# A modulation loaded by column halves, first products opened over them, and two operator groups moved to a later stage

## The chip, the cores and the metric

The kernel runs on one NeuronCore of a Trainium2 chip. The metric is device time in microseconds (us) of one execution. Engines are named as in the profile: PE multiplies matrices (PEld loads its weights), DVE, ACT and POOL work on tiles, SP only issues DMAs. ACT and POOL can issue DMAs too.

## The reference

Two transformer blocks run one after the other in fp32, on 256 tokens of width 1024. Only the first block's opening and the parameters of the second block's first mixer matter here.

```python
def first_block(x, c, ctx, c_ctx, ada_w, ada_b, g_mix, ...):
    ...
    for i in range(DEPTH):
        mod_lat = (silu_c @ ada_w[i] + ada_b[i])[:, None, :]
        mod_ctx = (silu_cc @ ada_w[i] + ada_b[i])[None, None, :]
        sh1, sc1, ga1, sh2, sc2, ga2 = jnp.split(mod_lat, 6, axis=-1)
        ...
        u_lat = modulate(rms_norm(h_lat, g_mix[i]), sh1, sc1)   # norm * (1 + sc1) + sh1
        u_ctx = modulate(rms_norm(h_ctx, g_mix[i]), csh1, csc1)
        if i % N_MIXERS == 0:
            ql, kl, vl = jnp.split((u_lat @ w).reshape(B, L, 3, H, dh), 3, axis=2)
            ql, qc = rms_norm(ql, na_q_gain[j]), rms_norm(qc, na_q_gain[j])
            ...
def s5_mixer(xn, w_in, lam_re, lam_im, b_re, b_im, c_re, c_im, d_skip, log_dt, w_glu):
    u = (xn @ w_in)
    a_bar = jnp.exp(lam * dt)
    b_bar = ((a_bar - 1.0) / lam)[..., None] * b_mat
    # scan: s = a_bar * s + b_bar u ;  y = Re(c_mat s) + d_skip * u ; then a gated product
```

## The kernel before

Activations lie transposed: feature tile k (128 of the 1024 features) has the latent tokens in `h[k]` and the context tokens in `hc[k]`, 256 columns each. Every fp32 operand is split in a high and a low part. For weights that is `whi` (ACT) and `wlo` (DVE), for activations `xh` (ACT) and `xl` (DVE). A product is three matmuls, `mm_x` or `mm_w`: high by high and the two mixed ones.

**The start stage** comes first. It works out the parameters of the second block's S5 mixer (class `S5`), loads and transposes the inputs, computes the shift and the scale of the first norm, norms, and splits the first weights. All of the S5 work needs only parameters, so the kernel does it where PE has little else.

- `S5.__init__` and `tables` are a serial chain of small DVE operations, with transposes on PE. `c` transposes the C matrices and copies them (`ct`, `pf`). It also builds the skip diagonal `dd`. There are four operator groups r = 0 to 3. `e(r)` builds group r's table on DVE from `pz` and `bb` through `tm`. `operators(r)` runs `k1` (`cbk` copies, products into `kp`, copied to `kt`), `et` (16 transposes, four copies, four DMAs into `edr`) and `k2` (transposes into `kst`). `save`, `k_out` and later `spread` write tables to DRAM (`cdr`, `kdr`, `tdr`). They are read again when the second block begins.
- `ada_steps(l, n)` computes modulation n (0 is shift, 1 is scale) of layer l. It has eight steps of one 512 KB row block each, and `ada(m)` runs the next m of the queue `ada_q`. The last step copies to `adacc`, transposes, and adds the bias into `mods`. For the scale it also makes `scg`.
- `rstd` sums squares on PE, takes a square root on ACT and a reciprocal on DVE, and spreads the result over the partitions. `normed` makes for each feature tile and each stream `t` (DVE), `xh` (ACT) and `xl` (DVE).

**Order.** Most of the start is inside `tc.manual_schedule`, in which each engine runs what is written, in the written order. From `w_first.append` on, a scheduler orders the instructions by its own estimate.

**After the start** comes the neighbourhood attention, stage attn0. Its first pair of heads (`lead`) makes query and key products in the PSUM buffers `g`, and the value products go to `sc`. These are 96 matmuls each. `norm(b)` then norms the heads on DVE (`ss`, `rq`, `ri`, `rt`, `qn`, `sp`), and `turn(b)` transposes them on PE into `pt`. The pool `at0`, in which these tiles lie, takes the memory of `pp`, the pool of the S5 tables, which is closed at the end of the start. **mlp0** is the first block's feed-forward. It runs one `ada_q` step between its tiles.

## Time and profile before

| what | value |
|---|---|
| runs | 1773.23 us median of 3 (1770.42 to 1775.66) |
| profiled execution | 1774.26 us, of which the span is 1772.5 us, mean granted PE clock 0.982 |
| PE | 1684.8 us busy, 95% of the span |
| DVE, ACT, POOL | 1177.6, 797.4 and 445.7 us |
| DMA | 286.57 MB, mean 162 GB/s |

PE is the busiest engine, and it is near full after the first slice of the span. The stage of the change is the first 105 us. There all engines wait for each other, so shares over the whole span say little about it. How to read the rows further down: a timeline row has the start, the length, the engine, the line, the tiles written and read, and in brackets the idle time just before with what ended it. "x16" is a run of 16 instructions in one row. A windows row lists busy times of PE, PEld, DVE, ACT and POOL in one stretch, with the granted PE clock (1.00 is 2.4 GHz), the DMA share, and GB/s.

### The profile page before, as it was taken

The numbers are of one execution on the slowest core, as the hardware profiler recorded it, in microseconds if no ns is written. First come the engines' busy times: TensorE is split into PE (matmuls) and PEld (weight loads), VectorE is DVE, ScalarE is ACT, GpSimd is POOL, SyncE is SP. The second block draws the span as 40 slices with busy tenths as digits, with TensorE's granted clock in tenths as the row PEclk, the third lists the DMA queues.
The fourth block names the chain that finished last, engine by engine and source line by source line (L and its number), as shares of the span: only waits on it lengthen the run. The fifth ranks groups of instructions, "written<-read, shape, count | busy, mean of one in ns | idle before, by whom it ended". The sixth has DMA issues, their size and how long they took to land. (4 is left out here: it accounts for less than half of the span.)

```text
span 1772.5 us, 33896 instructions
## 1 busy us (share of the span) xinstructions
PE 1684.8 (95%) x13257; PEld 1485.2 (84%) x13257; DVE 1177.6 (66%) x2412; ACT 797.4 (45%) x1463; POOL 445.7 (25%) x619
## 2 busy tenths in 40 slices
PE   6899999999999999998998999989899999999999
PEld 5687888876677777888878999979899999789998
DVE  6877777855545333447985756768577788957674
ACT  5544444434323131324674635536444465544453
POOL 4022112146897000040002000221431322424130
PEclk9899999999999999999999999999999999999999
DMA  9566455333766555332206666698459574335952
GB/s 283 180 161 193 123 153 169 91 112 130 238 197 214 160 173 151 87 95 72 84 25 167 189 187 186 209 310 228 129 149 247 146 224 143 108 103 166 233 160 90
DMA packets 428288, 286.57 MB, mean 162 GB/s; under 512 B 37513, under 2 KB 405336, under 8 KB 428128
## 3 DMA queue, kind: packets, MB, share of 16 engines
q1 hardware_dynamic: 422064, 271.53, 52.8%
q0 software_dynamic: 2800, 7.29, 1.3%
q10 hardware_dynamic: 3264, 5.59, 0.9%
q8 instruction: 104, 1.70, 0.4%
q14 instruction: 56, 0.46, 0.1%
HBM read 271.41 MB, written 17.15 MB: 163 GB/s over the span
## 5 line engine op out<-in xcount | busy, mean ns | idle before, releaser
L109 ACT ACTIVATE whi<-raw 128x1024 fp32r<-128x1024 f32 (+2 forms) x388 | 390.1, 1013 | 470.4 <-PE g L295 361.5
L112 DVE TENSOR_TENSOR wlo<-raw,whi 128x1024 fp32r<-128x1024 f32 (+2 forms) x388 | 466.1, 1207 | 186.3 <-ACT whi L109 182.7
L296 PE MATMUL g<-xh,wlo 128*128 128x256 f32 (+1 forms) x1216 | 372.8, 307 | 8.0 <-DVE wlo L112 8.0
L294 PE MATMUL g<-xh,whi 128*128 128x256 f32 (+1 forms) x1216 | 371.9, 307 | 1.6 <-ACT xh L109 1.2
L295 PE MATMUL g<-xl,whi 128*128 128x256 f32 (+1 forms) x1216 | 371.5, 305 | 0.0
L294 PE MATMUL g<-oh,whi 128*128 128x256 f32 (+1 forms) x1056 | 333.2, 316 | 3.5 <-ACT oh L109 1.4
L296 PE MATMUL g<-oh,wlo 128*128 128x256 f32 (+1 forms) x1056 | 333.0, 315 | 0.0
L295 PE MATMUL g<-ol,whi 128*128 128x256 f32 (+1 forms) x1056 | 332.6, 315 | 0.4 <-DVE ol L112 0.4
L296 PEld LDWEIGHTS g<-xh,wlo 128*128 128x128 f32 x1216 | 232.2, 191 | 21.5 <-DVE wlo L112 10.2
L294 PEld LDWEIGHTS g<-xh,whi 128*128 128x128 f32 x1216 | 231.6, 191 | 17.6 <-ACT whi L109 3.9
L295 PEld LDWEIGHTS g<-xl,whi 128*128 128x128 f32 x1216 | 231.8, 191 | 10.9
L294 PEld LDWEIGHTS g<-oh,whi 128*128 128x128 f32 x1056 | 198.2, 188 | 24.2 <-issue 3.7
L295 PEld LDWEIGHTS g<-ol,whi 128*128 128x128 f32 x1056 | 198.3, 188 | 15.8 <-DVE ol L112 1.2
L296 PEld LDWEIGHTS g<-oh,wlo 128*128 128x128 f32 x1056 | 199.4, 189 | 14.3 <-issue 0.2
L302 PE MATMUL g<-whi,xh 128*128 128x256 f32 x560 | 163.1, 292 | 3.9 <-ACT whi L109 1.6
L303 PE MATMUL g<-wlo,xh 128*128 128x256 f32 x560 | 157.9, 282 | 0.1
L304 PE MATMUL g<-whi,xl 128*128 128x256 f32 x560 | 156.9, 283 | 0.2 <-DVE xl L115 0.2
L115 DVE SCALAR_TENSOR_TENSOR h<-g,mods,h 128x256 f32<-128x256 f32 x64 | 30.9, 483 | 142.2 <-PE g L296 142.2
L302 PEld LDWEIGHTS g<-whi,xh 128*128 128x128 f32 x560 | 105.9, 189 | 12.8 <-issue 8.7
L109 ACT ACTIVATE oh<-t 128x256 fp32r<-128x256 f32 (+1 forms) x108 | 51.3, 482 | 124.4 <-DVE t L112 124.4
L303 PEld LDWEIGHTS g<-wlo,xh 128*128 128x128 f32 x560 | 105.9, 189 | 0.8 <-issue 0.3
L304 PEld LDWEIGHTS g<-whi,xl 128*128 128x128 f32 x560 | 105.4, 189 | 1.3 <-issue 0.8
(329 smaller groups left out, 2823.4 us busy)
## 6 DMA issues: line engine op xcount, KB each, us to landing
raw<-mlp_w SPq DMA_DIRECT2D x128, 512.0 KB, 4.3
ada<-ada_w SPq DMA_DIRECT2D x88, 512.0 KB, 5.0
raw<-ffn_w_up SPq DMA_DIRECT2D x88, 512.0 KB, 5.2
raw<-ffn_w_down SPq DMA_DIRECT2D x32, 384.0 KB, 3.8
raw<-ffn_w_down SPq DMA_DIRECT2D x32, 320.0 KB, 3.4
raw<-na_wqkv SPq DMA_DIRECT2D x32, 256.0 KB, 5.0
raw<-a_w_glu SPq DMA_DIRECT2D x16, 512.0 KB, 7.2
raw<-w_kv SPq DMA_DIRECT2D x16, 512.0 KB, 3.7
```

Of the source, the lines that this page charges most:

```text
L109: last[0] = A.activation(out=o, in_=i, func=f, **kw)
L112: (e or V).tensor_tensor(out=o, in0=a, in1=b, op=op)
L115: V.scalar_tensor_tensor(out=o, in0=a, scalar=s, in1=b, op0=op0, op1=op1)
L294: T.matmul(ps, lhsT=a, rhs=xh[k][:, s0:s1], start=first, stop=False)
L295: T.matmul(ps, lhsT=a, rhs=xl[k][:, s0:s1], start=False, stop=False)
L296: T.matmul(ps, lhsT=b, rhs=xh[k][:, s0:s1], start=False, stop=last_)
L302: T.matmul(ps, lhsT=xh[k][:, t0:t0 + 128], rhs=a, start=first, stop=False)
L303: T.matmul(ps, lhsT=xh[k][:, t0:t0 + 128], rhs=b, start=False, stop=False)
L304: T.matmul(ps, lhsT=xl[k][:, t0:t0 + 128], rhs=a, start=False, stop=last_)
```

## The change

- The first shift and scale come as halves of their columns (`ada_half`, 256 KB per step). The first halves of both serve feature tiles 0 to 3, the second halves tiles 4 to 7.
- The norm of tiles 0 to 3 and the query and key products over them are written ahead of the second halves. The value products over them are interleaved with the second scale half. Then follow tiles 4 to 7 and the rest of both products. `operators(0)` stands between the two. All this is now inside the manual schedule. PSUM buffers `g` and `sc` stay open from the start into attn0.
- `e(0)` stands ahead of the squares' sums, `c` and the skip diagonal (`skip`) behind them. `e(1)` and `operators(1)` stand behind the last lead product.
- Groups 2 and 3 go to mlp0, between steps of `ada_q`, with `k_out` and `spread` behind them. What they need (`bb`, `pz`, `kst`) is written to `cdr` in `save` and read again by `reload` before mlp0. `save`, `et`, `k_out` and `spread` issue their DMAs on POOL now, not on ACT and SP.
- The B matrices come in one DMA each and are transposed by 32 transposes, where before there were 32 transposes and 32 products.

```diff
--- before.py
+++ after.py
+    def ada_half(l, n, j, tiles):
+
+        acc = [None]
+
+        def step(k):
+            t = tiles(k)
+            c0 = n * 1024 + j * 512
+            dma(out=t, in_=I["ada_w"][l, k * 128:(k + 1) * 128, c0:c0 + 512])
+            if k == 0:
+                acc[0] = bank("x")
+            ps = acc[0]
+            for q in range(4):
+                T.matmul(ps[32 * q:32 * q + 32, 0:128], lhsT=sl[:, k, :], rhs=t[:, 128 * q:128 * q + 128],
+                         start=k == 0, stop=k == KT - 1)
+            if k < KT - 1:
+                return
+            cp(adacc[:, 0:128], ps[:, 0:128])
+            pt = bank("x")
+            T.transpose(pt[:, 0:128], adacc[:, 0:128], ident)
+            c = n * 8 + 4 * j
+            m = mods[l][:, c:c + 4, :]
+            tt(m, pt[:, 0:128].rearrange("p (q x) -> p q x", q=4)[:, :, 0:2],
+               adab[l][:, c:c + 4].unsqueeze(2).to_broadcast([128, 4, 2]), ADD)
+            if n == 1:
+                stt(scg[l][:, 0, 4 * j:4 * j + 4, :], m, 1.0,
+                    gmix[l][:, 4 * j:4 * j + 4].unsqueeze(2).to_broadcast([128, 4, 2]), ADD, MUL)
+
+        return [lambda k=k: step(k) for k in range(KT)]
...
+            if between:
+                between()
...
-                for j in range(2):
-                    b_ = bt[r][j].rearrange("g (p h) -> g h p", h=16)
-                    for h_ in range(16):
-                        o_ = pb[r][64 * j:64 * j + 64, 32 * h_:32 * h_ + 32]
-                        if j:
-                            T.matmul(o_, lhsT=b_[:, h_, :], rhs=ident[0:32, 0:32])
-                        else:
-                            T.transpose(o_, b_[:, h_, :], ident[0:32, 0:32])
+                b_ = bt[r].rearrange("g (n h) -> g h n", h=16)
+                for h_ in range(16):
+                    T.transpose(pb[r][:, 32 * h_:32 * h_ + 32], b_[:, h_, :], ident[0:32, 0:32])
...
         def save(self):
             for i in range(2):
-                dma_a(out=cdr[:, 512 * i:512 * i + 512], in_=self.ct[i].rearrange("p g h -> p (g h)"))
-            dma_a(out=cdr[:, 1024:1536], in_=self.pf_.rearrange("p r t g -> p (r t g)"))
-            dma_a(out=cdr[:, 1536:1632], in_=self.ph_.rearrange("p i g -> p (i g)"))
+                G.dma_start(out=cdr[:, 512 * i:512 * i + 512], in_=self.ct[i].rearrange("p g h -> p (g h)"))
+            G.dma_start(out=cdr[:, 1024:1536], in_=self.pf_.rearrange("p r t g -> p (r t g)"))
+            G.dma_start(out=cdr[:, 1536:1632], in_=self.ph_.rearrange("p i g -> p (i g)"))
+            for i in range(2):
+                c = cdr[:, 1632:3168].rearrange("p (r x) -> p r x", r=4)
+                G.dma_start(out=c[:, :, 128 * i:128 * i + 128], in_=self.bb[i].rearrange("p (r g) h -> p r (g h)", r=4))
+                G.dma_start(out=c[:, :, 256 + 64 * i:320 + 64 * i],
+                            in_=self.pw2[i].rearrange("p (r g) t -> p r (g t)", r=4))
+                G.dma_start(out=cdr[:, 3168 + 256 * i:3424 + 256 * i],
+                            in_=self.kst[i][:, 0:2].rearrange("p r q j x -> p (r q j x)"))
 
         def e(self, r):
+            t = self.fp.tile([128, 2048], F32, tag=("e1", "e2", "em", "em")[r], name="em").rearrange(
+                "p (i q j t h) -> p i q j t h", i=2, q=4, j=2, t=8)
+            self.em[r] = [t[:, i] for i in range(2)]
+            if r < 2:
+                bb, pw2 = [x_[:, 8 * r:8 * r + 8, :] for x_ in self.bb], [x_[:, 8 * r:8 * r + 8, :] for x_ in self.pw2]
...
-                dma_a(out=edr[:, 16 * q + 4 * r:16 * q + 4 * r + 4, :], in_=et)
+                G.dma_start(out=edr[:, 16 * q + 4 * r:16 * q + 4 * r + 4, :], in_=et)
...
         def k_out(self):
             for qh in range(2):
                 for s in range(8):
-                    dma(out=kdr[:, 32 * qh:32 * qh + 32, 7 + s, :],
+                    G.dma_start(out=kdr[:, 32 * qh:32 * qh + 32, 7 + s, :],
...
+    lead = ExitStack()
+    psum_pools(lead, g=2, sc=2)
...
-            psum_pools(s0, x=5, s=3)
-            ada_pool(s0)
+            psum_more(s0, x=3, s=1)
+            adh = s0.enter_context(tc.tile_pool(name="adh", bufs=12))
...
-            halves = lambda k: [stage("l", 2 * (k // 2) + j) for j in range(2)] if k % 2 else None
-            ada_q = ada_steps(0, 0, halves) + ada_steps(0, 1, halves)
+            half = lambda k: adh.tile([128, 512], F32, tag="ada", name="ada")
+            for n in range(2):
+                ada_q.extend(ada_half(0, n, 0, lambda k, n=n: stage("l", 4 * n + k // 2) if k % 2 else half(k)))
+            for n in range(2):
+                ada_q.extend(ada_half(0, n, 1, half))
...
-                for f in sloads[7:]:
+                for f in sloads[5:]:
+                    f()
+                for f in small_loads[15:-1]:
                     f()
                 s5.tables()
-                for f in small_loads[15:-1]:
-                    f()
+                s5.tiles(pp, spare)
+                s5.e(0)
+                act(small, h[KT - 2][:, 0:1], AF.Sqrt, bias=eps, scale=0.0)
                 ada(4)
+                between = [lambda: None] * 2 + [lambda: ada(1)] * 6
+                between[3] = lambda: (prep_vectors(va), ada(1))
+                r_ = rstd(512, 0, None, "s", lambda: between.pop(0)())
                 s5.c()
-                s5.e(0)
-                ada(2)
-                act(small, h[KT - 2][:, 0:1], AF.Sqrt, bias=eps, scale=0.0)
-                r_ = rstd(512, 0, None, "s")
-                prep_vectors(va)
-                ada(3)
+                s5.skip()
+                ada(6)
+                x = new_x(xa, "x", 512, 16, 16)
+
+                def norm_k(*ks):
+                    normed(x, r_, 512, lambda k, v: scg[0][:, 0, k, v:v + 1], lambda k, v: modcol(0, 0, k, v), ks)
+
+                def lead_mm(i, k):
+                    for b in range(2):
+                        for t in range(2):
+                            mm_x(lead_ps[i][b][:, t * 256:(t + 1) * 256], w_first[i], 0, 256, x, k, (2 * b + t) * 128,
+                                 k == 0 and t == 0, k == KT - 1 and t == 1)
+
+                norm_k(0)
+                w_first = [Weights(wpairs(w, D, 0), by_k=True)]
+                norm_k(1, 2, 3)
+                lead_ps = [[bank("g"), bank("g")], [bank("sc"), bank("sc")]]
+                for k in range(4):
+                    lead_mm(0, k)
+                    ada(2)
+                w_first.append(Weights(wcols(w, 2 * D, 256), by_k=True))
+                operators(0)
+                for k in range(4):
+                    ada(2)
+                    lead_mm(1, k)
+                norm_k(4, 5, 6, 7)
+                for i in range(2):
+                    for k in range(4, 8):
+                        lead_mm(i, k)
                 s5.e(1)
-                operators(0)
-                ada(2)
-                w_first = [Weights(wpairs(w, D, 0), by_k=True)]
-                ada(2)
-                s5.e(2)
+                operators(1)
                 small_loads[-1]()
                 stt(gna, gna, 0.125, swg[:, 208:272], MUL, MUL)
                 ts(gsw[0], gsw[0], 0.125, MUL)
-                operators(1)
-                ada(3)
-            w_first.append(Weights(wcols(w, 2 * D, 256), by_k=True))
-            x = new_x(xa, "x", 512, 16, 16)
-            normed(x, r_, 512, lambda k, v: scg[0][:, 0, k, v:v + 1], lambda k, v: modcol(0, 0, k, v))
-            operators(2)
-            s5.e(3)
-            operators(3)
-            s5.zero()
-            s5.save()
-            s5.k_out()
+                s5.zero()
+                s5.save()
...
-            psum_pools(s0, g=2, sc=2, pt=2, po=1, x=1)
+            psum_more(s0, pt=2, po=1, x=1)
...
-                    return [load, mm_all, lambda: norm(0), lambda: norm(1), lambda: turn(0), lambda: turn(1)]
+                    return [load, lambda: norm(0), lambda: norm(1), lambda: turn(0), lambda: turn(1)]
...
-            ada_q[2::5] = [lambda f=f, s=s: (s5.spread(s), f()) for s, f in enumerate(ada_q[2:42:5])] + ada_q[42::5]
+            at_ = {20: s5.skip, 26: lambda: s5.e(2), 38: lambda: s5.e(3), 47: s5.k_out}
+            for n, r in ((30, 2), (42, 3)):
+                for i, f in enumerate((s5.k1, s5.et, s5.k2)):
+                    at_[n + i] = lambda f=f, r=r: f(r)
+            for n, g_ in at_.items():
+                ada_q[n] = lambda f=ada_q[n], g_=g_: (f(), g_())
+            ada_q += [lambda s=s: s5.spread(s) for s in range(8)]```

The first place is DVE where the norm begins, before. `t` is the scaled tile, `xl` its low part; `h` and `hc` are the two streams.

```order
L115 SCALAR_TENSOR_TENSOR scg_74<-mods_72,vt 128x16
L112 TENSOR_TENSOR e_506<-tm_432,tm_433 128x512
L115 SCALAR_TENSOR_TENSOR t<-h_78,scg_74,s 128x256
L115 SCALAR_TENSOR_TENSOR t<-hc_102,scg_74,s 128x256
L115 SCALAR_TENSOR_TENSOR t<-h_79,scg_74,s 128x256
L115 SCALAR_TENSOR_TENSOR t<-hc_103,scg_74,s 128x256
L115 SCALAR_TENSOR_TENSOR xl_891<-t,mods_72,xh_883 128x256 x2
```

The same place, DVE, after:

```order
L115 SCALAR_TENSOR_TENSOR scg_74<-mods_72,vt 128x8
L115 SCALAR_TENSOR_TENSOR t<-h_78,scg_74,s 128x256
L115 SCALAR_TENSOR_TENSOR xl_643<-t,mods_72,xh_635 128x256
L115 SCALAR_TENSOR_TENSOR t<-hc_108,scg_74,s 128x256
L115 SCALAR_TENSOR_TENSOR xl_643<-t,mods_72,xh_635 128x256
L112 TENSOR_TENSOR wlo<-raw,whi 128x1024 x2
L115 SCALAR_TENSOR_TENSOR t<-h_79,scg_74,s 128x256
```

Four `t` stood ahead of the first `xl`; now each `xl` follows its own `t`, and between them lies one ACT operation, `xh`.

The second place is POOL at the end of the start, before: from the loads of small vectors to the first work of attn0 (`sp`).

```order
L203 DMA swg<-na_k_gain 128x64
L961 DMA rp<-na_rpb 120x2x31
L963 DMA rpad<-rp 120x256
L782 MEMSET z 128x112
L112 TENSOR_TENSOR sp<-qn,sp 128x256 x6
```

POOL after, with what each waits for (DMASW is the landing of one of POOL's own earlier DMAs); `edr<-et` belongs to `operators(1)`, `cdr` to `save`:

```order
L794 DMA edr<-et 128x512 [waits DMASW0_49,Activation_49]
L794 DMA edr<-et 128x512 [waits DMASW1_49,Activation_49]
L1025 DMA rpad<-rp 120x256 [waits DMASW2_49]
L806 MEMSET z 128x112 [waits DMASW7_49,DMASW3_49]
L737 DMA cdr<-ct_188 128x512
L737 DMA cdr<-ct_189 128x512 [waits DMASW4_49]
L738 DMA cdr<-pf 128x512 [waits DMASW5_49]
L739 DMA cdr<-ph 128x96 [waits DMASW6_49,DVE_49]
L742 DMA cdr<-bb_275 128x4x128
L743 DMA cdr<-pz_369 128x4x64 [waits DMASW0_49,Pool_49]
L745 DMA cdr<-kst 128x256 [waits DMASW1_49,Activation_49]
L742 DMA cdr<-bb_276 128x4x128 [waits DMASW2_49]
```

Ten table writes and eight `et` writes now stand in POOL's order ahead of attn0's first work, behind the memset `z`; two more follow the last row, `cdr<-pz_370` and `cdr<-kst`.

The third place is DVE at the first head norm of attn0 (`ss`), before and then after.

```order
L112 TENSOR_TENSOR tm_432<-pz_398,bb_310 128x512 [waits DVE_49]
L112 TENSOR_TENSOR tm_433<-pz_399,bb_309 128x512
L112 TENSOR_TENSOR e_507<-tm_432,tm_433 128x512 [waits DVE_49]
L513 TENSOR_REDUCE ss<-t 128x4 [waits DMASW1_49,DMASW0_49,DMASW4_49,DVE_49,DMASW5_49,PE_49,Activation_49]
L513 TENSOR_REDUCE ss<-t 128x4 x2
```

DVE after:

```order
L112 TENSOR_TENSOR wlo<-raw,whi 128x1024 [waits DMAHW3_49,Activation_49]
L112 TENSOR_TENSOR em<-tm 128x512 [waits DVE_49]
L115 SCALAR_TENSOR_TENSOR swg<-swg 128x64 [waits DMASW7_49,DMASW6_49]
L120 TENSOR_SCALAR swg<-swg 128x64 [waits DMASW3_49]
L547 TENSOR_REDUCE ss<-t 128x4 [waits DMASW3_49,DMASW2_49,DMASW4_49,DMASW1_49,DMASW5_49,DMASW0_49,DMASW6_49,DVE_49,DMAHW4_49,PE_49,DMAHW5_49,Activation_49,Pool_49]
L547 TENSOR_REDUCE ss<-t 128x4 x2
```

In both, `ss` stands behind the last table of `e` and waits for the last users of the memory of `pp`. After, these include DMAs of POOL's queue; the one named DMASW3 is `cdr<-pz_370`, the last but one of `save`.

## Rows read from the trace of the kernel before

**Rows 1.** Profile page: the span, and busy time and share of each engine.

```profile
span 1772.5 us, 33896 instructions
PE 1684.8 (95%) x13257; PEld 1485.2 (84%) x13257; DVE 1177.6 (66%) x2412; ACT 797.4 (45%) x1463; POOL 445.7 (25%) x619
```

**Rows 2.** Windows: stretch, length, busy PE PEld DVE ACT POOL, clock, DMA.

```profile
30.00:50.00 20.00, 12.68 (x142) 6.92 (x142) 13.48 (x26) 10.84 (x32) 2.83 (x5) 0.68 0.94 269
50.00:75.40 25.40, 20.31 (x240) 12.66 (x238) 22.84 (x39) 16.29 (x36) 0.00 (x0) 0.85 0.71 236
75.40:104.70 29.30, 27.89 (x267) 25.82 (x268) 25.70 (x75) 16.33 (x39) 1.81 (x3) 1.00 0.45 130
600.00:750.00 150.00, 150.00 (x748) 115.71 (x748) 58.91 (x84) 40.28 (x52) 0.00 (x0) 1.00 0.47 141
```

**Rows 3.** Timeline of DVE: first head norm of attn0.

```profile
98.20 1.07 DVE L513 TENSOR_REDUCE ss<-t 128x4 f32<-128x256 f32 x3 [2.52 <-ACT et L109]
```

**Rows 4.** Timeline of PE: the first turn of heads.

```profile
104.67 0.29 PE L1077 MATMUL pt<-idr,sp 128*128 128x128 f32 x2
```

**Rows 5.** Timeline of DVE: S5 chain, skip diagonal, first table, reciprocal.

```profile
19.63 0.69 DVE L112 TENSOR_TENSOR t<-s,sm 128x512 f32<-128x512 f32 x1 [1.83 <-PE s L619]
30.33 0.19 DVE L112 TENSOR_TENSOR ph<-sm 128x32 f32<-128x32 f32 x1
32.88 1.21 DVE L112 TENSOR_TENSOR dd<-dr,cst 32x1024 f32<-32x1024 f32 x1 [2.35 <-ACT dr L109]
34.02 1.27 DVE L112 TENSOR_TENSOR tm<-pz,bb 128x512 f32<-128x512 f32 x2
42.10 0.94 DVE L432 RECIPROCAL sd<-sd 128x128 f32<-128x128 f32 x1
```

**Rows 6.** Timeline of PE: transposes of `c`, and operators(0) from first to last.

```profile
27.67 2.17 PE L711 MATMUL s<-cst,ci 128*128 128x128 f32 x16
43.19 1.14 PE L439 MATMUL s<-sd,cst 128*128 128x128 f32 x8 [3.14 <-DVE sd L432]
48.86 1.08 PE L752 MATMUL s<-e,cbk 128*32 128x128 f32 x16
54.62 0.44 PE L775 MATMUL s<-cst,kt 128*128 128x128 f32 x2 [0.34 <-ACT et L109]
```

**Rows 7.** Timeline of DVE: weight split, first and last of the norm.

```profile
57.52 2.36 DVE L112 TENSOR_TENSOR wlo<-raw,whi 128x1024 fp32r<-128x1024 f32 x2 [1.07 <-DMA edr<-et]
73.08 0.47 DVE L115 SCALAR_TENSOR_TENSOR t<-h,scg,s 128x256 f32<-128x256 f32 x1
87.34 0.87 DVE L115 SCALAR_TENSOR_TENSOR xl<-t,mods,xh 128x256 fp32r<-128x256 f32 x2
```

**Rows 8.** Timeline of ACT: one high part of the norm.

```profile
74.92 0.51 ACT L109 ACTIVATE xh<-t,mods 128x256 fp32r<-128x256 f32 x1
```

**Rows 9.** One line's instructions: POOL's issue of a 256 KB write (ns, min/median/max).

```profile
L845 POOL DMA_DIRECT2D fdr<-fm x16: 714/717/752, 465.6 to 567.2; - x16
```

**Rows 10.** DMA issues: queue, count, KB each, median us to landing.

```profile
edr<-et ACTq DMA_DIRECT2D x16, 256.0 KB, 2.8
fdr<-fm POOLq DMA_DIRECT2D x16, 256.0 KB, 3.7
ci<-a_c_im POOLq DMA_DIRECT2D x2, 256.0 KB, 9.9
```

**Rows 11.** Groups by line, PE, 0 to 105 us: the four operator groups.

```profile
L767 PE MATMUL s<-cst,e 128*128 128x128 f32 x64 | 12.8, 341 | 1.2 <-ACT et L109 1.0
L752 PE MATMUL s<-e,cbk 128*32 128x128 f32 x128 | 7.8, 322 | 3.1 <-ACT cbk L109 2.3 <-DVE e L112 0.7
L756 PE MATMUL s<-cst,dd 32*32 32x16 f32 x64 | 2.1, 196 | 0.0
L775 PE MATMUL s<-cst,kt 128*128 128x128 f32 x8 | 1.8, 301 | 0.8 <-ACT et L109 0.8
```

**Rows 12.** Timeline of SP: the writes of `k_out`.

```profile
99.38 12.09 SPq L790 DMA_DIRECT2D kdr<-kst  x16
```

More of the change, by code (lines that the diff above doesn't have):

```diff
@@ L419, in square_sum, with rstd_rows @@
                 yield acc
-    def rstd_rows(n, pooled=6, late=KT - 2):
+    def rstd_rows(n, pooled=6, late=KT - 2, between=None):
         w = n // 4
@@ L464, in gained, with normed @@
             stt(view(x[1][k]), h[k], g, view(x[0][k]).bitcast(F32), MUL, SUB)
-    def normed(x, r, n, gain, shift=None):
+    def normed(x, r, n, gain, shift=None, ks=range(KT)):
         xh, xl = x
-        for k in range(KT):
+        for k in ks:
             t = tmp_tile()
@@ L647, in __init__ @@
             self.pw = pw = [pp.tile([128, 9, 32], F32, name=f"pw{i}") for i in range(2)]
-            cbs = spare(5, "cbk")
-            G.memset(cbs, 0.0)
-            self.cbk = [cbs[:, 256 * i:256 * i + 256].rearrange("p (q a b h) -> p q a b h", q=4, a=2, b=2)
-                        for i in range(2)]
             G.memset(pw[0][:, 0, :], 1.0)
@@ new lines, in reload, with tiles @@
+            G.dma_start(out=self.cb, in_=cdr[:, 2400:3168])
+            self.tiles(fp, lambda i, nm: fp.tile([128, 512], F32, tag=f"{nm}{i}", name=nm))
+            for i in range(2):
+                G.dma_start(out=self.kst[i][:, 0:2].rearrange("p r q j x -> p (r q j x)"),
+                            in_=cdr[:, 3168 + 256 * i:3424 + 256 * i])
+        def tiles(self, fp, get):
+            self.fp = fp
+            self.em, self.kt = [None] * 4, [None] * 4
+            self.ett = lambda q: get((0, 1, 4, 15)[q], "et")
+            self.tm = [get(2 + i, "tm").rearrange("p (n t h) -> p n t h", n=4, t=8) for i in range(2)]
+            cbs = get(5, "cbk")
+            G.memset(cbs, 0.0)
+            self.cbk = [cbs[:, 256 * i:256 * i + 256].rearrange("p (q a b h) -> p q a b h", q=4, a=2, b=2)
+                        for i in range(2)]
+            self.kst = [get(10 + i, "kst").rearrange("p (r q j x) -> p r q j x", r=4, q=2, j=2) for i in range(2)]
+            self.dr = fp.tile([32, 32], F32, name="dr")
+            G.dma_start(out=self.dr, in_=I["a_d_2"][0].rearrange("(a b) -> a b", b=32))
+            self.dd = fp.tile([32, 32, 32], F32, name="dd")
@@ new lines, in skip, with reload2 @@
+        def skip(self):
+            pdk = bank("x")
+            T.transpose(pdk[0:32, 0:32], self.dr, ident[0:32, 0:32])
+            act(self.dr, pdk[0:32, 0:32], AF.Copy)
+            tt(self.dd, self.dr.unsqueeze(2).to_broadcast([32, 32, 32]),
+               ident[0:32, 0:32].unsqueeze(1).to_broadcast([32, 32, 32]), MUL)
+        def reload2(self, fp):
+            c = fp.tile([128, 608], F32, name="cp")
+            tt(c[:, 0:1], h[KT - 1][:, 0:1], hc[KT - 1][:, 0:1], ADD, G)
+            dma(out=c, in_=cdr[:, 1024:1632])
+            self.pf = c[:, 0:512].rearrange("p (r t g) -> p r t g", r=2, t=8)
+            self.ph = c[:, 512:608].rearrange("p (i g) -> p i g", i=3)
```

102 lines of the change are left out of this document (46 added, 56 removed).

## The prediction

> **What bounds the kernel now.** I read the page first: PE is busy for 95% of a span of 1772.5 us [rows 1]. A gain can therefore only come from the stretch in which PE lacks work, and work put where PE is full costs its whole time. The windows show both places. From 30 to 50 us PE works 12.68 of 20 us at a granted clock of 0.68, and up to 75.4 us it works 20.31 of 25.4 us at 0.85. In the window from 600 to 750 us, inside mlp0, it works 150.00 of 150 us [rows 2]. Next come the timelines. The event that starts PE's steady feed is the first turn of heads at 104.67 us [rows 4]. By then all 192 lead products are done. The turn follows 6.5 us behind the first head norm `ss`, which starts at 98.20 us, and `ss` had waited 2.52 us for the last `et` copy of `operators(3)` [rows 3]. That wait is the key to this change. The tiles of the head norm take the memory of the S5 tables, so `ss` can't start before the tables' last reader is done. The windows also say who is full before that: DVE works 22.84 of 25.40 us and 25.70 of 29.30 us [rows 2].
>
> So the question is when `ss` starts in the changed kernel, and what the moved groups cost in mlp0. I follow the written order of the engines from step to step, with durations from the trace.
>
> **The head of the start: shorter.** The S5 chain ends with `ph` at 30.5 us. DVE no longer waits 1.83 us for the products of the B matrices [rows 5], since 32 of them are gone: about 28.5. `e(0)` now follows at once. It took 8.1 us (34.02 to 42.10) [rows 5]: 36.6. Behind it stand vectors, half a modulation, square root, reciprocal (0.94) [rows 5] and its spread (1.14) [rows 6]. Before, the reciprocal started with `e(0)`'s end, and its spread ended 2.2 us later. With the vectors and the modulation now ahead of it, 5.8 us is my estimate: 42.4. Then `c` and `dd`, which took from 27.67 to 34.09, 6.4 us [rows 5, 6]. Half a microsecond of that was other work, so 5.9: 48.3. With the last small steps of the scale (1.3, an estimate), the first norm starts at **49.6 us**, where it started at 73.08 [rows 7]. So far 23.5 us are gained. The halves themselves aren't late, since the DMAs had a share of 0.94 busy until 50 us [rows 2] and half of the bytes are wanted first.
>
> **The norm: slower per tile.** Before, eight tiles took from 73.08 to 88.2, 1.9 us each, because several `t` ran ahead while ACT made `xh`. Now `t`, `xh` and `xl` follow each other: 0.47 [rows 7], 0.51 [rows 8], 0.43 (half of 0.87) [rows 7] and a few hundredths between engines, 1.45 us for a stream and 2.9 for a tile. Four tiles and the split of the query weights (2.36 for two) [rows 7], part of which waits for `whi`: 14.6, so 64.2.
>
> **Between the halves: DVE waits for PE.** The first products and the shift's second half take PE to about 66, and the value weights' split takes DVE to 69.2. `operators(0)` took 6.2 us (48.86 to 55.06) [rows 6], from 67 to 73 now. The scale's second half is written behind it, interleaved with value products: 6.3 us, and 1 for the copy, transpose and `scg`. So the norm's second half starts at 80.3 us. Four tiles and one more weight split take it to 92.7.
>
> **The tail: everything in a row.** `e(1)` (8.1) and two more weight splits (2.36) end at 103.1 us. Before, this table's work lay beside PE's early operators. The rest of `operators(1)` follows: 5.3 of its 6.2, as some `cbk` copies can go ahead: **108.4 us**. The lead products, at 99.4, are done earlier.
>
> **The save on POOL: the new wait.** `ss` now waits also for POOL's writes from `pp`. POOL issues in order: the `et` writes, then a memset that waits for the second of them to land, then ten writes, of which `cdr<-pz_370` is the ninth. The second `et` is issued near 106. The nearest row is POOL's `fdr` write of 256 KB, issue 0.72 [rows 9], landing 3.7 [rows 10]: memset at 110.3. Nine issues of 0.6 on average (most writes are smaller): 115.8. Landing again: **ss at 119.5 us**. Bounds: with the landing of ACT's `et` (2.8) [rows 10] and quick issues 117; with that of the `ci` loads on POOL's queue (9.9) [rows 10], which shared their time with loads, 132. I take 3.7 because those are also writes to DRAM from POOL in an otherwise light stretch. The Trainium skill, "DMA: Bandwidth & Descriptors", section "Anatomy of one DMA — SWDGE (gpsimd) path", gives 2 us plus the bytes at 436 GB/s, an estimate of 2.6 us here; the row shows 3.7, and the two landings by the page would make the sum 2.2 us smaller.
>
> The turn follows 6.5 us behind `ss` at most, and I take 6, as ACT and the weights are ahead by then: 125.5. **PE's steady feed starts 20.8 us later than before.** Behind the waiting `ss` stand all of DVE's work for attn0 and the weight splits for the next pair; ACT's value copies, POOL's first bias work and PE's turn wait for the same writes, so nothing fills the hole.
>
> **Operators 2 and 3 in mlp0.** All four groups took 12.8 + 7.8 + 2.1 + 1.8 = 24.5 us of PE [rows 11], 6.1 each, partly at the low clock of the start. At the full clock 4 each is my estimate, as 0.68 and 0.85 [rows 2] were granted for most of that time: +8. The bound above is 12.2, the one below 0 if PE's waits there take them in, against which stands 150.00 of 150 [rows 2]. `e(2)` and `e(3)` cost nothing: DVE is busy 58.91 of 150 there, and ACT 40.28 [rows 2] takes in the copies. SP loses 12.09 us of `kdr` writes [rows 12] in front of the bias loads. That is worth nothing for the turn, perhaps 1 us behind it, and the same writes cost POOL nothing in mlp0, where it is idle [rows 2].
>
> **The sum.** 20.8 + 8.0 = 28.8 on the profiled execution's 1774.26 us, so 1803. That execution stands 1.0 above the median of the three runs, so 1802.
>
> **Rivals.**
> - A longer hold: `save`'s writes land like the `ci` loads, `ss` at 128 to 132. For it: ten writes and eight `et` writes on one queue. Against: the DMAs have little else then. 1811 to 1825.
> - A low clock. The granted clock was 0.68 where PE worked 12.68 of 20 us [rows 2], and the new order has PE wait between groups of 12 products. If the 8.5 us of PE work on the path that I took at full clock ran at 0.68, it would take 12.5: +4, inside my range. The Trainium skill, "TensorE: Matmul & The Clock Gate", section "HAM oscillation — how this bites in real kernels", says that waits between short groups of matmuls bring the slow clock back every time, which speaks against opening products piecewise; the window's 0.68 agrees.
> - A smaller loss: quick landings (117) and half of the groups hidden in mlp0. 1784 to 1795.
> - No hold: `ss` needs only the query and key products, at 95.5, and the tail, the save and `e(1)` lie in its shade. The turn at 101.5 and +8 in mlp0 give 1778; 1772 to 1784. Against: the order of DVE has `ss` behind `e(1)`, and the waits named there.
> - Faster: DVE's work sets the start, not its waits. Its work ahead of the turn falls by `e(2)` and `e(3)`, 16.3 us. If DVE stays as full as it was (22.84 of 25.40), the turn comes at 88.4, and with +8 in mlp0 the time is 1766. It decides from the point where `ss` starts before 85 us (98.2 less 8 and less 0.3% of the time). Against: 11 us of idle DVE between the halves, and the tail.
>
> **How the numbers follow.** Forecast (1795 to 1811) 52%, longer hold 20%, smaller loss 16%, no hold 7%, faster 5%. The range 1786 to 1820 leaves out about 2 in 10: no hold, faster, a little of the smaller loss and the top of the longer hold. A measurement of this kernel tells 0.3%, about 5.3 us, from no change. Faster by more than that 5%, within 4% (half of no hold), slower 91%.
>
> **What would show it.** After: the first `t` near 50 us; `t` and `xl` alternating at 1.45 us; a hole on DVE from 70 to 80; `operators(1)` ending near 108; `ss` near 119 with an idle time of 10 us or more that a DMA from `cdr` or ACT ended; the turn near 125; PE's busy time in mlp0 longer by 8. I'm wrong if `ss` starts before 105 us, or if mlp0 isn't longer.

## The result and the profile after

The changed kernel takes 1801.74 us, median of 4 runs (1800.18 to 1805.69), against 1773.58 us (1770.42 to 1775.66, 4 runs) for the kernel before. The ratio is 1.0159, 95% interval 1.0142 to 1.0177: 28 us slower. The forecast was 1802. Medians and ratios further down leave out two slow runs: one of 2162.68 us of the kernel with the tail in the hole, and one of 7041.31 us of the kernel before, taken beside the last two experiments.

The profiled execution took 1805.69 us, 3.95 above its median and the slowest of the four. The page and the windows of the kernel after, columns as in [rows 1] and [rows 2]:

```profile
span 1803.9 us, 34073 instructions
PE 1689.0 (94%) x13322; PEld 1489.6 (83%) x13322; DVE 1182.5 (66%) x2418; ACT 798.7 (44%) x1464; POOL 488.0 (27%) x677
```

```profile
30.00:50.00 20.00, 10.08 (x107) 7.87 (x107) 8.80 (x19) 4.81 (x13) 0.00 (x0) 0.66 0.59 192
50.00:75.40 25.40, 21.77 (x258) 17.53 (x259) 12.85 (x22) 12.32 (x23) 2.16 (x4) 0.87 0.63 207
...
104.70:125.80 21.10, 3.23 (x15) 2.18 (x13) 6.33 (x39) 4.57 (x13) 11.04 (x19) 0.58 0.73 210
600.00:750.00 150.00, 149.99 (x857) 114.43 (x857) 58.15 (x88) 40.11 (x57) 20.32 (x32) 1.00 0.62 189
```

PE's busy sum rose by only 4.2 us, so most of the 31.4 us of span is time in which PE had nothing to do. The third window here is the new one: 3.23 us of PE work in 21.1 us. Up to 75.4 us DVE was busy 22.84 of 25.40 us [rows 2], and is busy 12.85 now: the earlier norm did not make the engines fuller, but emptier.

Where the time lies is found by landmarks that both traces have: the first turn of heads, and the reciprocals `sd` that open each later norm. Between them:

| stretch | before | after | difference | forecast |
|---|---|---|---|---|
| start to first turn | 104.7 | 124.5 | +19.8 | +20.8 |
| first turn to second reciprocal (attn0) | 304.9 | 299.2 | -5.7 | 0, perhaps -1 |
| second to third (mlp0) | 398.7 | 411.2 | +12.5 | +8 |
| third to fourth | 152.5 | 151.1 | -1.4 | 0 |
| fourth to fifth (second block, its mixer) | 307.0 | 312.9 | +5.9 | 0 |
| fifth to the end | 504.7 | 505.0 | +0.3 | 0 |

The timeline of DVE after, from the S5 chain to the first head norm:

```profile
25.20 0.25 DVE L112 TENSOR_TENSOR ph<-sm 128x32 f32<-128x32 f32 x1
...
37.96 0.95 DVE L466 RECIPROCAL sd<-sd 128x128 f32<-128x128 f32 x1 [1.70 <-ACT sd L109]
...
48.85 0.48 DVE L115 SCALAR_TENSOR_TENSOR t<-h,scg,s 128x256 f32<-128x256 f32 x1
49.90 0.48 DVE L115 SCALAR_TENSOR_TENSOR xl<-t,mods,xh 128x256 fp32r<-128x256 f32 x1 [0.57 <-ACT xh L109]
...
73.42 1.23 DVE L112 TENSOR_TENSOR wlo<-raw,whi 128x1024 fp32r<-128x1024 f32 x1 [5.45 <-ACT whi L109]
76.85 0.29 DVE L125 COPY adacc<-x 128x128 f32<-128x128 f32 x1 [2.20 <-PE x L394]
...
78.02 0.48 DVE L115 SCALAR_TENSOR_TENSOR t<-h,scg,s 128x256 f32<-128x256 f32 x1
...
90.43 1.29 DVE L112 TENSOR_TENSOR tm<-pz,bb 128x512 f32<-128x512 f32 x2
...
119.47 1.07 DVE L547 TENSOR_REDUCE ss<-t 128x4 f32<-128x256 f32 x3 [18.60 <-DMA cdr<-kst]
```

The norm begins at 48.85, where it began at 73.08 [rows 7]. Each `xl` waits for its `xh`, and the next `t` starts 1.45 us after the last. The second half begins at 78.02 behind a hole of DVE. `e(1)` begins at 90.43, and the first head norm `ss` at 119.47, where it began at 98.20 [rows 3]; its wait grew from 2.52 to 18.60 us. The bracket names `kst`, the write that landed last, at 119.19. By the order of DVE `ss` waits for the `pz` write ahead of it, which landed at 118.86, 0.61 us before `ss` began. In the three experiments that leave `save` where it is on POOL this distance is 0.60 or 0.61 us too, and in one of them `ss` began before `kst` had landed. POOL in the same time, and ACT and PE that wait with DVE:

```profile
108.55 0.19 POOL L806 MEMSET z<- 128x112 f32 x1
109.00 1.08 POOL L737 DMA_DIRECT2D cdr<-ct  x2 [0.26 <-issue]
...
113.92 0.75 POOL L743 DMA_DIRECT2D cdr<-pz  x1
114.66 0.55 POOL L745 DMA_DIRECT2D cdr<-kst  x1
```

```profile
119.16 1.21 ACT L109 ACTIVATE vv<-sc 128x256 f32<-128x256 f32 x4 [11.78 <-DMA cdr<-pz]
```

```profile
106.20 0.43 PE L799 MATMUL x<-cst,kt 128*128 128x128 f32 x2
124.50 0.47 PE L1148 MATMUL pt<-idr,sp 128*128 128x128 f32 x2 [17.87 <-DVE sp L112]
```

The tables' last work on PE starts at 106.20. POOL issues the save from 109.00 to 115.2, the writes land, and only then do DVE and ACT go on. PE idles 17.87 us.

### The profile page after: what moved, and what is told of

It reads as the page before. It is cut to its first block, busy times and chain, and to the rows that moved or that the text cites. A ratio compares the mean times of both kernels' runs of the same rounds, so it can differ in the third digit from the quotient of the medians.

```text
span 1803.9 us, 34073 instructions
## 1 busy us (share of the span) xinstructions
PE 1689.0 (94%) x13322; PEld 1489.6 (83%) x13322; DVE 1182.5 (66%) x2418; ACT 798.7 (44%) x1464; POOL 488.0 (27%) x677
## 5 line engine op out<-in xcount | busy, mean ns | idle before, releaser
L109 ACT ACTIVATE whi<-raw 128x1024 fp32r<-128x1024 f32 (+2 forms) x388 | 389.8, 1013 | 467.6 <-PE g L298 326.5
L112 DVE TENSOR_TENSOR wlo<-raw,whi 128x1024 fp32r<-128x1024 f32 (+2 forms) x388 | 466.8, 1208 | 177.5 <-ACT whi L109 166.5
L299 PE MATMUL g<-xh,wlo 128*128 128x256 f32 (+1 forms) x1216 | 374.0, 308 | 8.2 <-DVE wlo L112 8.2
L298 PE MATMUL g<-xl,whi 128*128 128x256 f32 (+1 forms) x1216 | 372.7, 306 | 0.0
L298 PE MATMUL g<-ol,whi 128*128 128x256 f32 (+1 forms) x1056 | 332.7, 315 | 0.4 <-DVE ol L112 0.4
L299 PE MATMUL g<-oh,wlo 128*128 128x256 f32 (+1 forms) x1056 | 333.0, 315 | 0.0
L299 PEld LDWEIGHTS g<-xh,wlo 128*128 128x128 f32 x1216 | 232.9, 192 | 21.5 <-DVE wlo L112 10.4
L298 PEld LDWEIGHTS g<-xl,whi 128*128 128x128 f32 x1216 | 232.5, 191 | 11.3 <-issue 0.4
L299 PEld LDWEIGHTS g<-oh,wlo 128*128 128x128 f32 x1056 | 199.7, 189 | 14.4 <-issue 0.2
L298 PEld LDWEIGHTS g<-ol,whi 128*128 128x128 f32 x1056 | 198.5, 188 | 15.6 <-DVE ol L112 1.1
L115 DVE SCALAR_TENSOR_TENSOR h<-g,mods,h 128x256 f32<-128x256 f32 x64 | 30.8, 483 | 144.1 <-PE g L299 144.0
L109 ACT ACTIVATE oh<-t 128x256 fp32r<-128x256 f32 (+1 forms) x108 | 51.3, 482 | 134.7 <-DVE t L112 134.7
## 6 DMA issues: line engine op xcount, KB each, us to landing
raw<-na_wqkv SPq DMA_DIRECT2D x32, 256.0 KB, 4.2
```

Of the source, the lines that this page charges most:

```text
L109: last[0] = A.activation(out=o, in_=i, func=f, **kw)
L112: (e or V).tensor_tensor(out=o, in0=a, in1=b, op=op)
L115: V.scalar_tensor_tensor(out=o, in0=a, scalar=s, in1=b, op0=op0, op1=op1)
L298: T.matmul(ps, lhsT=a, rhs=xl[k][:, s0:s1], start=False, stop=False)
L299: T.matmul(ps, lhsT=b, rhs=xh[k][:, s0:s1], start=False, stop=last_)
```

## The experiments

The theory is: `ss` waits in a row for the tail (`e(1)`, `operators(1)`) and for POOL's writes from the S5 tables, since the head norm's tiles take the tables' memory; and the groups in mlp0 cost PE their whole time.

**Save early.** What `save` writes is ready by 50 us, except `kst`. The edit moves those writes, and the write of the padded bias table, ahead in the program.

```
                 s5.skip()
+                small_loads[-1]()
+                s5.save()
                 ada(6)
...
                 operators(1)
-                small_loads[-1]()
...
-                s5.save()
+                s5.save_kst()
```

> The changed kernel with one thing moved: the writes of ct, pf, ph, bb and pz to cdr and the bias row write (rpad) stand on POOL right behind the skip diagonal, not behind operators(1); only the two kst writes stay at the end. Theory of the hold (the first head norm ss waits 18.6 us for POOL's queue of writes from the memory that it takes): ss then waits for operators(1) alone and starts at 107 to 108 us instead of 119.5, the first turn comes near 113.5 instead of 125.8, and the time falls by 10 to 12 us, to about 1790. Rival, the tail itself (e(1), operators(1) and the et writes in a row set ss, the save lies in their shade): less than 4 us. Rival, slow landing on POOL's queue wherever the writes stand: ss still near 119, no change.

Measured: 1790.19 us (1787.07 to 1794.56), ratio 1.0103 [1.0080, 1.0127]. DVE:

```profile
107.29 1.07 DVE L547 TENSOR_REDUCE ss<-t 128x4 f32<-128x256 f32 x3 [6.11 <-PE x L802]
```

`ss` now follows the last transpose of `operators(1)`, 12.2 us earlier, and the turn comes at 112.15, 12.3 us earlier. The two ratios differ by 0.0056, or 10 us. The hold by the writes is shown, with its size; one of the moved writes, the bias table's, comes back in a later experiment.

**The same save on ACT's queue.** Only the issuing engine changes; the place in the program stays.

```
         def save(self):
             for i in range(2):
-                G.dma_start(out=cdr[:, 512 * i:512 * i + 512], in_=...)
+                dma_a(out=cdr[:, 512 * i:512 * i + 512], in_=...)
...
```

> The changed kernel with the ten writes of save issued by ACT instead of POOL, at the same place of the program. If the hold is made of POOL's ten slow issues (0.54 to 0.77 us each) and its slow landing (5.2 us), ACT's issues at 0.33 us and landing at 2.8 us put ss at about 113.5 us, 6 us earlier, and the time at about 1796. If only the place in the order counts (writes behind operators(1), whoever issues them): ss at 117 to 119 and a gain under 2 us.

Measured: 1801.72 us (1795.38 to 1801.91), ratio 1.0155 [1.0130, 1.0181].

```profile
117.71 1.07 DVE L547 TENSOR_REDUCE ss<-t 128x4 f32<-128x256 f32 x3 [17.06 <-DMA cdr<-pz]
```

ACT begins 3.4 us sooner than POOL did, but takes 9.6 us for the ten issues where POOL took 6.2. `ss` comes 1.8 us earlier, where the place in the program made 12.2. Which queue writes is of little account; when the program asks for the writes decides.

**The tail in DVE's hole.** On top of the early save, `e(1)` goes ahead of `operators(0)`, and the three parts of `operators(1)` between the tiles of the norm's second half.

```
+                s5.e(1)
                 operators(0)
...
-                norm_k(4, 5, 6, 7)
+                norm_k(4)
+                s5.k1(1)
+                norm_k(5)
+                s5.et(1)
+                norm_k(6)
+                s5.k2(1)
+                norm_k(7)
...
-                s5.e(1)
-                operators(1)
```

> The early save of the first experiment, and in addition e(1) stands ahead of operators(0), where DVE was idle between the two halves of the norm, and operators(1) is interleaved with the norm of tiles 4 to 7. Theory (the tail in a row costs the rest of the loss in the start): ss starts behind the last query and key product, near 96.5 us, the turn near 102.5, another 11 us earlier than with the early save alone: about 1779. Rival, the copies of operators(1) on ACT delay the norm's high parts by as much as is gained: ss at 104 or later and less than 4 us gained on the early save.

Measured: 1783.02 us (1781.31 to 1785.70, three runs), ratio 1.0063 [1.0043, 1.0083]. The turn came at 106.04, 6.1 us earlier than with the early save alone, where about 10 were expected. DVE and PE of this kernel show what took the rest:

```profile
85.89 0.48 DVE L115 SCALAR_TENSOR_TENSOR xl<-t,mods,xh 128x256 fp32r<-128x256 f32 x1 [2.04 <-ACT xh L109]
...
94.89 0.75 DVE L547 TENSOR_REDUCE ss<-t 128x4 f32<-128x256 f32 x2
99.81 0.42 DVE L547 TENSOR_REDUCE ss<-t 128x4 f32<-128x256 f32 x1 [3.96 <-ACT t L109]
```

```profile
96.72 0.63 PE L363 MATMUL x<-ada,sl 128*32 128x256 f32 x4 [2.71 <-DMA ada<-ada_w]
```

The tables' copies on ACT now stand ahead of `xh`, so the norm pays for them; the first `ss` is early, but its second half waits, through ACT's `t`, for query and key products that PE does late; a modulation step that waited 2.71 us for its load stands among them. The tail's place matters, and the norm's `t`, `xh`, `xl` in single file is the next limit.

**The norm skewed.** On top of that, `t` and `xh` of a tile are written ahead of `xl` of the tile before, and the query and key products of tiles 4 to 6 each ahead of a part of `operators(1)`.

```
-                norm_k(1, 2, 3)
+                for k in (1, 2, 3):
+                    norm_a(k)
+                    norm_b(k - 1)
+                norm_b(3)
...
+                norm_a(4)
+                for k, f in ((4, s5.k1), (5, s5.et), (6, s5.k2)):
+                    norm_a(k + 1)
+                    norm_b(k)
+                    lead_mm(0, k)
+                    f(1)
```

> The third experiment (early save, tail in the hole) with the norm written skewed: both t of tile k+1 stand ahead of both xl of tile k, so that ACT's xh runs beside DVE; and each query and key product over tiles 4 to 7 stands behind its own tile, ahead of the next piece of operators(1). Theory (the written order t, xl, t, xl costs 0.9 us per tile, as 0.58 us of idle time stands before each xl): the norm takes 1.9 to 2.0 us per tile instead of 2.9, ss starts at 86 to 88 us and the turn comes at 92 to 96 instead of 106: 1770 to 1776, level with the kernel before. Rival, the second half of the scale (PE and its DMAs) paces the second half of the norm: ss at 91 or later, less than 5 us gained.

Measured: 1772.71 us (1767.75 to 1776.26, 10 runs), ratio 0.9999 [0.9985, 1.0014]: level with the kernel before. Its DVE, and PE where the second half of the scale ends:

```profile
53.84 0.47 DVE L115 SCALAR_TENSOR_TENSOR t<-h,scg,s 128x256 f32<-128x256 f32 x1
55.42 0.47 DVE L115 SCALAR_TENSOR_TENSOR t<-h,scg,s 128x256 f32<-128x256 f32 x1
...
65.21 0.29 DVE L125 COPY adacc<-x 128x128 f32<-128x128 f32 x1 [5.76 <-PE x L394]
...
77.65 0.69 DVE L112 TENSOR_TENSOR em<-tm 128x512 f32<-128x512 f32 x1
78.26 0.28 DVE L125 COPY adacc<-x 128x128 f32<-128x128 f32 x1
79.42 0.48 DVE L115 SCALAR_TENSOR_TENSOR t<-h,scg,s 128x256 f32<-128x256 f32 x1
...
92.52 1.07 DVE L547 TENSOR_REDUCE ss<-t 128x4 f32<-128x256 f32 x3 [0.73 <-POOL z L809]
```

```profile
76.15 0.64 PE L394 MATMUL x<-ada,sl 128*32 128x128 f32 x16
78.68 0.30 PE L400 MATMUL x<-cst,adacc 128*128 128x128 f32 x1 [1.89 <-DVE adacc L125]
```

A tile takes 1.6 us instead of 2.9 in the first half. But the second half still begins at 79.42, so `ss` came at 92.52, later than expected, and the turn at 99.08, 5.6 us earlier than in the kernel before. The time is as expected, but the steps to it are not: the rival had `ss` at 91 or later. What paces the second half is the written order of PE: the shift's half is summed behind the first query and key products (DVE waits 5.76 us for it), the scale's last step stands behind the value products and ends at 76.8; then `e(1)`, moved ahead here, keeps DVE until 78.26. Neither the 5.6 us at the turn nor the 8.7 that attn0 is shorter here (296.2 us) reach the end: mlp0 takes 408.4 us, 9.7 more than before, and the second block's mixer 312.8, 5.8 more.

**The groups in mlp0, twice and not on PE.** One kernel runs `k1`, `et` and `k2` of group 2 a second time. In another, groups 2 and 3 do nothing on PE.

```
+            for i, f in enumerate((s5.k1, s5.et, s5.k2)):
+                at_[33 + i] = lambda f=f: f(2)
```

> The changed kernel with the operators of group 2 (k1, et, k2) run a second time in mlp0, with the same result written again. From the reciprocal of the second norm to that of the third, mlp0 and what lies around it took 398.7 us before and 411.2 after, 12.5 more for two groups and the skip diagonal. Theory (a group costs PE its full time there, 4 us by the prediction, up to 6.1 by the bound): the stretch grows by 4.0 to 6.2 us and the time is 1806 to 1808. Rival, the 12.5 us are something else (reloads and POOL's writes in the way of weight loads, e on DVE): less than 3 us more.

```
-                for i, f in enumerate((s5.k1, s5.et, s5.k2)):
+                for i, f in enumerate((lambda r: None, s5.et_sbuf, s5.k2_sbuf)):
```

> The changed kernel, but k1, et and k2 of groups 2 and 3 do nothing on PE: products and transposes of these two groups are left out, et's eight writes go out from the table em, and kst's entries are copies of em, so DMAs and tables e(2) and e(3) stay. Theory: these groups cost their whole PE time in mlp0, 4 us each, so mlp0's stretch (second to third reciprocal) falls from 411.2 to 402 to 404 us and the time by 7 to 9, to 1793 to 1795. Rival: PE's waits in mlp0 take the groups in, and the rest of mlp0's +12.5 comes from elsewhere: the stretch stays over 408 and the time within 3 us of 1802. The extra 6 us in the second block (fourth to fifth reciprocal, 312.9 against 307.0 us before) have nothing to do with the groups by the theory, and stay within 1 us of 312.9.

Measured: twice, 1801.99 us (1800.22 to 1805.38), ratio 1.0177 [1.0160, 1.0194]; off PE, 1791.41 us (1790.08 to 1796.37), ratio 1.0095 [1.0076, 1.0114]. The first was expected to take 4 to 6 us more and by its time can't be told from the changed kernel: the ratio is higher by 0.0018, or 3 us, with intervals that overlap. The second is lower by 0.0064, or 11 us. The traces are finer. All four have 1536 products into `g` between the second and the third reciprocal. The time of the n-th of them behind its reciprocal, less the same in the kernel before, in us:

| product | after | group 2 twice | groups off PE |
|---|---|---|---|
| 180 | 3.4 | 0.1 | 1.7 |
| 660 | 4.1 | 0.8 | 2.0 |
| 900, behind group 2 | 7.9 | 8.9 | 2.0 |
| 1200, behind group 3 | 11.9 | 12.9 | 3.7 |

Group 2 costs 3.8 us once, 8.1 twice and nothing off PE; group 3 costs 4.0. Off PE a delay of 1.8 us is left between these two rows. It lies ahead of the place of group 3, in waits that the changed kernel doesn't show: 0.9 us around a modulation step that waits for its load, and 0.9 around a product that waits for its low part `ol`.

```profile
683.71 0.64 PE L363 MATMUL x<-ada,sl 128*32 128x256 f32 x8 [0.70 <-DMA ada<-ada_w]
```

Nothing of the groups is taken in by waits of PE: around them (from 600 to 735 us after, and from 480 to 715 before) PE has no wait that is marked. The first 180 products are late by 0.1 to 3.4 us in kernels whose instructions there are the same, so that part is not the groups' doing, and the second run of group 2 is offset by it in the stretch (412.2 us, against 411.2 after). The groups by line, PE after, between the two reciprocals (lines 791 and 776 answer to 767 and 752 of [rows 11], two groups instead of four; the small products with `dd` and the transposes of `kt` add 1.0 and 0.9 us):

```profile
L791 PE MATMUL x<-cst,em 128*128 128x128 f32 x32 | 4.2, 279 | 0.0
L776 PE MATMUL x<-em,cbk 128*32 128x128 f32 x64 | 2.5, 276 | 0.0
```

**Why attn0 got shorter.** The stretch behind the first turn fell by 5.7 us, and my only term for it was SP's 12.09 us of `kdr` writes [rows 12], at 1 us. Three kernels put 16 writes of half the size back on SP: behind the save of the changed kernel, behind the early save with the tail in the hole, and behind the early save with the bias table written late, so that no bias load can pass them. The diff is that of the third, against the changed kernel; the method stands in all.

```
+        def k_half(self):
+            for qh in range(2):
+                for s in range(8):
+                    dma(out=kdr[:, 32 * qh:32 * qh + 16, 7 + s, :],
+                        in_=self.kst[qh][16 * s:16 * s + 16, 0:2]...)
...
                 s5.skip()
+                s5.save()
                 ada(6)
...
                 operators(1)
                 small_loads[-1]()
...
-                s5.save()
+                s5.save_kst()
+                s5.k_half()
```

> The changed kernel with 16 small writes put back on SP at the end of the start (kst of groups 0 and 1 into kdr, half of the bytes of the kernel before; they are written again later, so nothing changes in the output). From the first turn to the second norm's reciprocal the kernel before took 304.9 us, the changed one 297.9. Theory that the 12.09 us of these writes on SP, in front of bias loads and modulation loads, were the reason: 4 to 7 us slower, 1806 to 1809. Rival, that PE's waits there went because DVE and ACT had the next weights split ahead of the late turn: 0 to 1 us.

> The third experiment with 16 writes of kst on SP at the end of the start, so that SP issues them in front of the bias loads with no hold to hide them (in the earlier run with such writes SP was done 2 us ahead of the late turn). From the turn to the second norm's reciprocal the third experiment took 299.0 us, the kernel before 304.9. Theory that SP's 12 us were the reason: the bias loads start 11 to 14 us later, PE waits for the first softmax, and the stretch from the turn grows by 4 to 6 us. Rival, the reason is DVE's and ACT's load ahead of the turn: the stretch stays within 1.5 us of 299.0.

> Early save as in e1, but the padded bias table is written behind operators(1) again, and 16 writes from kst to kdr (half the size) stand on SP behind the last of save, ahead of all bias loads. Those loads then begin about 7 us behind the first turn, as in the kernel before. What is open: why the stretch from the first turn of heads to the second reciprocal takes 299.2 us in the changed kernel and 304.9 before, where I forecast that SP's freed 12 us are worth perhaps 1. Theory SP: the late bias loads make PE wait in attn0's first 75 us; here the stretch takes 303 to 306, first turn 112 to 113, time 1793 to 1796. Rival (the stretch is shorter because DVE and ACT have less other work around the turn): the stretch takes 298 to 301 as in e1, time 1789 to 1792.

The first expectation has 297.9 us for the stretch in the changed kernel; counted from the first turn at 124.50, as here, it is 299.2. Measured, in this order: 1797.73 us, ratio 1.0140 [1.0120, 1.0160], stretch 298.1 us; 1779.33 us, ratio 1.0040 [1.0027, 1.0052], 296.0 us; 1793.82 us, ratio 1.0111 [1.0096, 1.0126], 297.9 us. The stretch was never longer, so nothing speaks for SP. But none of the three put the loads where they stood before. There, SP issued the first two at 112.25, 7.6 us behind the turn. In the first kernel they began at 122.28, ahead of a turn at 124.20; in the second, two loads slipped ahead of the writes. In the third, SP wrote as planned, and the turn moved instead:

```profile
110.96 9.48 SPq L823 DMA_DIRECT2D kdr<-kst  x16
120.68 5.25 SPq L1209 DMA_DIRECT2D bt<-rpad  x8
```

```profile
114.25 1.07 DVE L547 TENSOR_REDUCE ss<-t 128x4 f32<-128x256 f32 x3 [13.48 <-DMA cdr<-kst]
```

```profile
rpad<-rp POOLq DMA_DIRECT2D x1, 120.0 KB, 6.8
```

The turn came at 119.06 instead of 112 to 113, because `ss` began 7.0 us later than with the early save. The bracket names a `kst` write, but `ss` waits for no semaphore of the first of the two, and the second landed at 116.2, behind the start of `ss`. What fits is the bias table's write (DMA issues, 100 to 125 us), which this kernel leaves behind `operators(1)`: issued at 106.88, it landed at 113.67, and `ss` began 0.58 us behind it, as it begins 0.6 us behind `pz` in the changed kernel. It would be the hold of this change once more, by a single late write, but no run moves this write alone. So the cause of the 5.7 us stays open. What can be read is what PE waited for in the kernel before, in this stretch, and waits for no longer:

```profile
128.49 0.38 PE L1143 MATMUL sc<-a,q 128*128 128x256 f32 x1 [2.21 <-ACT p L109]
...
150.69 0.50 PE L302 MATMUL g<-whi,xh 128*128 128x256 f32 x2 [1.63 <-ACT whi L109]
```

All of PE's waits for ACT there come to 4.8 us: softmax (`p`, 3.2) and a weight split (1.6). In the trace of after, PE has no wait that is marked from the first turn to 210 us. That ACT and DVE got ahead while everything waited for the save would fit, but it was not tried.

## Why the prediction was right, point by point

**The mechanism is the one forecast, at its place.** The head of the start came out at 48.85 for the first `t` (49.6). The S5 chain ended 3 us earlier than I had it (25.4 against 28.5), and this was lost again further on: the spread and the 16 transposes of `c` ran at the low clock (2.07 and 3.90 us, where [rows 6] has 1.14 and 2.17). The pace of the norm was 1.45 us per stream, as worked out. The second half began at 78.02 (80.3) and `operators(1)` ended at 107.4 (108.4).

**The save.** `ss` was forecast at 119.5 and came at 119.47, with two errors that cancel. The `et` writes landed in 2.8 us, not 3.7, so the memset stood at 108.55, not 110.3, and the ninth write was issued by 114.7, not 115.8. From there it took 4.8 us to `ss`, where I had 3.7: 4.2 to the landing, and 0.6 from the landing to `ss`, which I had at nothing. The row I chose counts from the start of an issue, and I added the issue to it; its 3.7 us are 3.0 behind the end of the issue. It is also of single writes; these ten followed each other. Landing times:

```profile
edr<-et POOLq DMA_DIRECT2D x4, 256.0 KB, 2.8
...
cdr<-bb POOLq DMA_DIRECT2D x2, 256.0 KB, 5.3
cdr<-pz POOLq DMA_DIRECT2D x2, 128.0 KB, 5.1
```

(DMA issues of after, 100 to 126 us; the last number is the median time from the start of an issue to the landing.) The 2.6 us that I had worked out for 256 KB from the Trainium skill, "DMA: Bandwidth & Descriptors", section "Anatomy of one DMA — SWDGE (gpsimd) path", agrees with the first row and is half of the second: it is a price for one transfer, not for the last of ten.

**The turn** was +19.8, not +20.8. It followed `ss` by 5.0 us, where I took 6. Two slips of the working did no harm: four tiles and a weight split from 80.3 end at 93.1, not 92.7, and the time for "faster" is 1765 with the 1.0 us of the median, not 1766.

**mlp0** was +12.5, not +8. The groups' 4 us each hold (3.8 and 4.0), and they are not hidden. The rest lies ahead of them, 3.4 us by product 180 and 0.7 up to 660, and I had no term for it; in the ten changed kernels, whose instructions are the same up to product 180, it is 0.1 to 3.7 us there. In this trace 2.3 of the 3.4 arise in one place. PE waits 3.56 us for a modulation's `adacc`, where it waited 2.83 before, and the eight products behind it start 0.43 us apart, at the low clock, where it was 0.23 before:

```profile
474.67 0.49 PE L370 MATMUL x<-cst,adacc 128*128 128x128 f32 x2 [3.56 <-DVE adacc L125]
```

Of the 0.7, 0.3 is a product of the skip diagonal, which the changed kernel builds once more in mlp0.

**attn0** was the term that was mis-sized most: -5.7 where I had perhaps -1, and the engine I named, SP, isn't shown to be the cause.

**The second block** had no term and shows +5.9. DVE's instructions stand there in the order of before; what differs is PE's clock. The window of 10 us that begins 245 us behind the fourth reciprocal, in the kernel before, after, and with the writes on SP ahead of the bias loads (columns as in [rows 2]):

```profile
1206.00:1216.00 10.00, 8.95 (x79) 8.75 (x78) 7.93 (x14) 5.62 (x16) 0.13 (x2) 1.00 1.18 287
```

```profile
1231.00:1241.00 10.00, 7.28 (x81) 6.64 (x82) 7.13 (x10) 4.84 (x15) 0.00 (x0) 0.66 1.19 291
```

```profile
1224.00:1234.00 10.00, 8.89 (x78) 8.52 (x74) 8.73 (x16) 6.23 (x18) 0.13 (x2) 1.00 1.20 291
```

The granted clock is 1.00, 0.66 and 1.00, and the whole stretch takes 307.0, 312.9 and 307.9 us. In the eleven profiles of this study the five with 0.66 in this window take 310.6 to 312.9 us (after, save early, tail in the hole, norm skewed, group 2 twice), one with 0.83 takes 309.8, and the five with 1.00 take 307.0 to 310.0. So after, 3 to 6 us of this stretch go with the clock (312.9 against 310.0 and 307.0). The kernel with the groups off PE, whose stretch was expected within 1 us of 312.9, is one of those with 1.00 (310.0). PE after, ahead of the window and in it:

```profile
1231.34 0.89 PE L1687 MATMUL g<-sw,sst 64*32 64x128 f32 x43 [1.11 <-DVE sst L112]
1234.61 0.64 PE L1687 MATMUL g<-sw,sst 64*32 64x128 f32 x5 [2.39 <-issue]
...
1235.56 0.42 PE L298 MATMUL g<-gl,whi 128*128 128x256 f32 x1
1235.77 0.42 PE L299 MATMUL g<-gh,wlo 128*128 128x256 f32 x1
...
1239.80 0.28 PE L298 MATMUL g<-gl,whi 128*128 128x256 f32 x1
1239.92 0.28 PE L299 MATMUL g<-gh,wlo 128*128 128x256 f32 x1
```

PE had waited for `sst` and for nothing that the profile shows (2.39 us), ran at 1.2 GHz, with a product every 0.21 us, and later at 2.4 GHz, with one every 0.12. With one profile per kernel I can't tell what decides whether the clock falls: the kernel, by the phase in which it gets there, or the execution. That stays open.

**The sum.** Against 28.8 the errors of the terms are -1.0 (start), -5.7 (attn0), +4.5 (mlp0), -1.4, +5.9 (second block) and +0.3: together +2.6 in this execution, which lies 3.95 above its median. The two terms that carry the forecast were good to 1 us (the turn) and to 0.2 us (the groups). That the rest nearly cancels is luck, and the sum is better than its parts.

**The rivals.** The longer hold fell with `ss` at 119.47, no hold with the wait of 18.60 us, and the smaller loss with both, as the groups aren't hidden either. Faster was to need `ss` before 85; the best rearranged kernel reached 92.52, and is level with the kernel before. The clock in the new hole was 0.58, and 0.66 from 30 to 50 us; the low clock is in the sum above.

## What to carry to other kernels

A tile that takes over memory waits for the last reader of the old one, and a DMA that writes the old tile out is such a reader: ask for the write as soon as its data is there, since its place in the program counts (12.2 us here) far more than its queue (1.8). Before a load is halved to open work earlier, follow the written order of the next engines: here 24 us gained at the norm became 20 lost at the turn, because the norm went into single file and everything behind it, the save last, stood in a row. Work moved into a stage where PE is full costs its whole time there (4 us a group), so the stage it leaves must give back more.
